# A modulation section summed on TensorE in four column groups instead of on VectorE

## The chip, the core and the metric

The kernel runs on one core of one Trainium2 chip. A core has five engines that run their own instruction streams in order: TensorE (PE in the profile; PEld is its loading of weights), VectorE (DVE), ScalarE (ACT), GpSimd (POOL) and SyncE (SP), which issues most DMAs. The metric is the device time of one execution, in microseconds.

## The reference

One decoder layer for 256 tokens of width 2048, batch 1, all in float32. Six vectors of 2048 numbers, shift, scale and gate for each of two halves, are made from a conditioning vector c ("the modulation"); this product with the 2048 x 12288 matrix `w_ada` is what the change touches.

```python
mod = einsum("bd,de->be", silu(c), w_ada) + b_ada
shift1, scale1, gate1, shift2, scale2, gate2 = split(mod, 6)
h = rms_norm(x, norm1_g) * (1 + scale1) + shift1
proj = einsum("bsd,de->bse", h, w_in)              # 73 column tiles of 128
lru_out = gelu(proj_gate) * rg_lru(conv(proj_x), ...)        # 32 of the tiles
ssd_out = mamba2_heads(proj_z, proj_xBC, proj_dt, ...)       # 41 of the tiles
mix = einsum("bse,ed->bsd", concat(lru_out, ssd_out), w_out)
x = x + gate1 * mix
h2 = rms_norm(x, norm2_g) * (1 + scale2) + shift2
x = x + gate2 * peer(h2, ...)                      # product keys, 16384 experts, top 16
out = rms_norm(x, final_norm_g)
```

`rg_lru` is a depthwise convolution, two small gate products per head and a scan along the tokens. `mamba2_heads` is a convolution, a chunked state-space scan in four groups of heads, and a gated norm.

## The kernel before, in words

Activations lie with features on the 128 partitions and tokens along the free axis. Every weight matrix comes from HBM as 512 KB blocks of 128 x 1024 numbers (`raw`, four buffers). ScalarE makes the rounded high part of a block (line 144), VectorE the low part, the block less its high part (line 153), both into `hl` (four buffers), and TensorE multiplies high and low parts. `issue_split` (line 139) queues ScalarE's part of one block and, one block behind, VectorE's, and after that the DMA of a further block on SP. It is called once after each half tile of products, so a block's split starts when TensorE has freed the buffer four blocks back.

The kernel runs in stages, on TensorE in this order:

1. Shift and scale of the first half of the layer (`ada_group`, line 250): 512 KB pieces of `w_ada` are the moving operand, `silu(c)` the stationary one. `cz` holds each column of `silu(c)` widened with zeros to 32 columns, and four products with four different 128-row pieces go to the four 32-row groups of one PSUM bank (line 257). ScalarE then copies the bank (line 266), and four products with a column of ones add up its rows and bring the result into column form (line 271). The first 12 tiles of the input projection run in between (`w_pass`).
2. The loop over the other 61 tiles of the input projection (line 795): 32 tiles of the SSD part first (slots 0 to 31), then 29 of the LRU part (slots 32 to 60). Each tile has two halves of 8 row blocks; tiles in which the high part of the weights meets both parts of `h` in one 512-column product use `wide` (lines 444 and 446), the others three products of 256 columns (lines 809 to 811).
3. The output projection: its first half by `w_out` rows (lines 869 to 871), its second half by column tiles (lines 915 and 916), with the first gate applied in `x2_evac` (line 838). Then the second norm, the query product, product keys and top 16, and the experts (a dense part by TensorE, the rest gathered by GpSimd).

The order of the side work is written by hand. `mid()` (line 170) runs once after each half tile and queues what was deferred for it; `bg_pop()` runs once after a tile and queues one step of the SSD or LRU work (its TensorE part at once, its elementwise part at the next `mid`). In the SSD part these steps are transposes, state and output products (lines 523 to 650), and in the first and middle tiles a softplus of many small VectorE instructions (lines 202 to 215); in the LRU part the gate products (line 663), the convolution (lines 417 and 421), scans (line 697) and gated outputs.

The other sections of the modulation are summed on VectorE while the projections run. `adq` (line 354) lists 96 steps: three sections (index 2, the first gate; 3 and 4, scale and shift of the second half), two halves of 1024 columns, 16 row blocks each. `ada_step` (line 373) multiplies one 128 x 1024 block of `w_ada` by a column of `silu(c)` and adds it to the running sum `adacc` (line 384; the first of a sum on line 381), then queues on SP the DMA of a further block (line 364; two buffers). After 16 steps, eight products with ones (line 393) bring the sum into column form two slots later. `ada_tick(rate, slot)` adds the rate to a counter and does one step for each whole number in it. It is called once for each tile of the loop from slot 1 on, with 0.65 in the SSD part and 1.1 in the LRU part, and 60 times in the output projection with 0.74. The last section, the second gate, is made later and is not touched.

Of the kernel before, what the change touches and what calls it, by code (L numbers as in the profile page):

```python
# [8 lines left out]
FT = mybir.dt.float32  # L9
# [5 lines left out]
AF = mybir.ActivationFunctionType  # L15
# [4 lines left out]
D = 2048  # L20
# [7 lines left out]
NRAW = 4  # L28
NHL = 4
GD = 3  # L30
ADA_SSD, ADA_LRU, ADA_OUT = 0.65, 1.1, 0.74

N0 = 12
NQ = 4
# [24 lines left out]
def hybrid_kernel(ctx, tc, xT, cols, w_ada, w_in, lru_w, w_o1, w_o2, w_q, keys, u_t, v_t, fng, out):  # L59
    nc = tc.nc  # L60
    pe, act, dve, pool, sp = nc.tensor, nc.scalar, nc.vector, nc.gpsimd, nc.sync
# [7 lines left out]
    mix = mixs.enter_context(tc.tile_pool(name="mix", bufs=1))  # L69

    def bank(n):
        return psum.tile([128, 512], FT, name=f"b{n}")
# [13 lines left out]
    def col(name, i=0, n=1):  # L86
        o, w = COLS[name]
        return cc[:, o + i:o + i + n]
# [3 lines left out]
    ones = const.tile([128, 128], FT, name="ones")  # L92
# [46 lines left out]
    def issue_split():  # L139
        n = st["split"]  # L140
        if n < len(items):
            r = raws.pop(n)
            t = wp.tile([128, 2, 1024], FR, name="hl", bufs=NHL)
            act.activation(t[:, 0], r, AF.Copy)  # L144
            hls[n] = t
            st["split"] += 1
            los.append((t, r))
        issue_lo(st["lag"] if n < len(items) else 0)
# [7 lines left out]
    def take():  # L156
        n = st["use"]
        st["use"] += 1
        return hls.pop(n)
# [7 lines left out]
    def defer(f, d=0):  # L167
        stages[d].append(f)

    def mid():  # L170
        fs = stages.pop(0)
        stages.append([])
        for f in fs:
            f()

    def bg_pop():
        for q in (bg, bg2):
            if q:
                pf, ef = q.pop(0)[:2]
                if pf:  # L180
                    pf()
                if ef:
                    defer(ef)
# [34 lines left out]
    cact = const.tile([128, 16], FT, name="cact")  # L218
# [9 lines left out]
    mod = const.tile([128, 6, 16], FT, name="mod")  # L228
# [122 lines left out]
            mid()  # L351


    adq = [(s, h, k) for s in (2, 3, 4) for h in range(2) for k in range(16)]
    ada = {"dma": 0, "use": 0, "acc": None, "bank": 6}
    adr = {}

    def ada_dma():
        n = ada["dma"]
        if n < len(adq):  # L360
            s, h, k = adq[n]
            adr[n] = mix.tile([128, 1024], FT, name="adr", bufs=2)
            o = {2: 2, 3: 4, 4: 3, 5: 5}[s] * D + h * 1024
            sp.dma_start(adr[n], w_ada[k * 128:(k + 1) * 128, o:o + 1024])
            ada["dma"] += 1
# [3 lines left out]
    def pe_due(slot):  # L369
        while pedue and pedue[0][0] <= slot:  # L370
            pedue.pop(0)[1]()

    def ada_step(slot):
        u = ada["use"]
        if u >= len(adq):
            return
        s, h, k = adq[u]
        w = adr.pop(u)
        if k == 0:
            ada["acc"] = mix.tile([128, 1024], FT, name="adacc", bufs=2)  # L380
            dve.tensor_scalar(ada["acc"], w, cact[:, 0:1], None, op0=OP.mult)
        else:
            a = ada["acc"]
            dve.scalar_tensor_tensor(a, w, cact[:, k:k + 1], a, op0=OP.mult, op1=OP.add)  # L384
        ada["use"] += 1
        ada_dma()
        if k == 15:
            a = ada["acc"]

            def fin():  # L390
                p = bank(ada["bank"])
                for i in range(8):
                    pe.matmul(p[:, i:i + 1], a[:, i * 128:(i + 1) * 128], ones[:, 0:1], start=True, stop=True)

                def add():
                    m = mod[:, s, 8 * h:8 * h + 8]
                    dve.tensor_add(m, p[:, :8], col("b_ada", 16 * s + 8 * h, 8))
                    if s == 3:
                        dve.scalar_tensor_tensor(m, m, 1.0, col("g2", 8 * h, 8), op0=OP.add, op1=OP.mult)
                defer(add)  # L400
            pedue.append((slot + 2, fin))
# [3 lines left out]
    def ada_tick(rate, slot):  # L405
        adt[0] += rate
        while adt[0] >= 1.0:
            adt[0] -= 1.0
            ada_step(slot)
# [32 lines left out]
    def wide(ps, w, kk, x, k):  # L442
        c = slice(kk * 128, (kk + 1) * 128)
        pe.matmul(ps, w[:, 0, c], x[:, k].rearrange("p a b -> p (a b)"), start=(k == 0), stop=False,  # L444
                  skip_group_check=True)
        pe.matmul(ps[:, :256], w[:, 1, c], x[:, k, 0], start=False, stop=(k == 15), skip_group_check=True)  # L446
# [276 lines left out]
    def lru_w_load():  # L723
        nonlocal nw
        if nw < 16:
            t = mix.tile([128, 2, 128], FT, name="wai", bufs=2)
            sp.dma_start(t, lru_w[nw])
            LR["w"][nw] = t
            nw += 1
# [57 lines left out]
    mid()  # L787
    mid()
    mid()
    for _ in range(2):  # L790
        ada_dma()
    for n in range(n2):
        w_pass(3, n, lambda e, ps: defer(lambda: evac(ETILES[e], ps)))
    slot = 0
    for e in ETILES[N0:]:
        ps = bank(slot % 3)
        two = e < 16 or 32 <= e < 48
        if not two:
            ps = ps[:, :256]
        for h in range(2):  # L800
            w = take()
            for kk in range(8):
                k = 8 * h + kk
                wh = w[:, 0, kk * 128:(kk + 1) * 128]
                wl = w[:, 1, kk * 128:(kk + 1) * 128]
                if two:
                    wide(ps, w, kk, hT, k)
                    continue
                pe.matmul(ps, wh, hT[:, k, 0, :], start=(k == 0), stop=False)  # L809
                pe.matmul(ps, wh, hT[:, k, 1, :], start=False, stop=False)  # L810
                pe.matmul(ps, wl, hT[:, k, 0, :], start=False, stop=(k == 15))  # L811
            issue_split()
            mid()
            if h == 0 and slot > 0:
                ada_tick(ADA_SSD if e >= 32 else ADA_LRU, slot)
        if e == 62:
            for _ in range(2):
                lru_w_load()
        bg_pop()
        ada["bank"] = 6 if slot >= 44 else (slot + 2) % 3  # L820
        pe_due(slot)
        defer(lambda e=e, ps=ps: evac(e, ps))
        slot += 1
# [38 lines left out]
    for n, k in enumerate(korder):  # L862
        w = take()
# [41 lines left out]
    for d in range(8, 16):  # L905
        ps = bank(3 + d % 2)
        for q in range(4):
            w = take()
            for kk in range(8):
                k = korder[8 * q + kk]  # L910
# [108 lines left out]
    for tb in range(2):  # L1019
        a = s1.tile([128, 1800], FT, name=f"ts{tb}")  # L1020
# [179 lines left out]
    for q in range(4):  # L1200
        w = [take() for _ in range(NQ // 2)]
        for kk in range(4):
            k = 4 * q + kk
# [11 lines left out]
    for e in range(NQ, 16):  # L1215
        p = bank(4 + e % 2)
# [381 lines left out]
```

## Time and profile before

| | |
|---|---|
| median of 3 runs | 2150.16 us (2148.74 to 2153.45) |
| the profiled execution | 2152.05 us, span 2150.3 us |
| input projection loop, SSD part | 147.2 to 366.0 us of the span |
| input projection loop, LRU part | 366.0 to 571.7 us |
| output projection and second norm | about 571.7 to 772 us |

The span runs from the first instruction of the program to the last; the execution's time has some 1.7 us around it. Three kinds of view are used below. In busy time by stretch, each engine has its busy microseconds and number of instructions in a stretch of the span; PEclk is TensorE's granted clock as a share of full speed, and the last two columns are the busy share of the DMA engines and the GB/s that they moved. In the timeline, a row is a start, a duration, an engine, the line in the kernel, the operation, and output and inputs by name; a number in square brackets is idle time of that engine just before, and what ended it. Rows of one line that follow each other are merged, with their count. Products overlap on TensorE, so a product's cost in a dense sequence is the distance between starts, not its duration. In the waits, a row names who waited for whom, with total, number and longest. A float32 product is two instructions in the profile.

### The profile page before, as it was taken

To read this page: it belongs to the slowest core of one execution; us is meant where nothing else is said; L and a number is where in the kernel's file an instruction comes from. 1 tells how busy PE (TensorE), PEld (TensorE's weight loads), DVE (VectorE), ACT (ScalarE), POOL (GpSimd) and SP (SyncE) were. 2 spreads that over 40 slices of the span, in tenths; PEclk is the share of its full clock that TensorE was granted. 3 is DMA by queue.
4 is the path that set the end of the run, shared out by engine and by line. 5 is a ranking of instruction groups with operands and counts; after the bars stand their busy time and mean duration, and the time that the engine had idled before them with its cause. 6 is when DMAs were issued, how large, how long until landed. Compare 5 with 4: busy or idle time off the path is not lost.

```text
span 2150.3 us, 34720 instructions
## 1 busy us (share of the span) xinstructions
PE 2074.9 (96%) x13028; PEld 1629.3 (76%) x13028; DVE 1396.2 (65%) x1995; ACT 965.7 (45%) x1468; POOL 886.2 (41%) x729
## 2 busy tenths in 40 slices
PE   7999999999999989999999999999999999999997
PEld 4789898988999888888788787766666656656663
DVE  2368887987878867879979996443343354344344
ACT  3346665666644454444345454333333333333332
POOL 0003243322212010000515661678777767767774
PEclk9999999999999999999999999999999999999998
DMA  9967666767789955568786778899999999999996
GB/s 371 387 235 251 214 213 229 255 222 257 260 289 322 344 175 174 190 222 268 241 264 225 243 252 280 279 368 351 340 364 352 359 353 342 374 368 359 355 355 241
DMA packets 250615, 620.54 MB, mean 289 GB/s; under 512 B 38024, under 2 KB 122168, under 8 KB 228152
## 3 DMA queue, kind: packets, MB, share of 16 engines
q1 hardware_dynamic: 188992, 387.76, 52.4%
q0 software_dynamic: 45056, 175.52, 22.0%
q10 hardware_dynamic: 16400, 55.06, 7.6%
q8 instruction: 102, 1.67, 0.3%
q14 instruction: 65, 0.53, 0.1%
HBM read 696.60 MB, written 14.72 MB: 331 GB/s over the span
## 4 chain that ended last, share of the span: by engine, by line
PE 62%; DVE 15%; DMA 13%; issue 5%; ACT 2%; POOL 1%; SPq 0%; POOLq 0%; DVEq 0%; ACTq 0%
PE b L444 11%; PE b L1436 10%; PE b L1350 9%; DVE hl L153 7%; PE b L446 5%; DMA raw<-in_w_in 4%; PE b L1276 3%; PE b L1278 3%; PE b L1277 3%; PE b L915 3%; DMA two<-in_w_ada 3%; DMA vq<-in_v_t,X 2%; DMA X<-ad,X 2%; PE b L809 2%; PE b L811 2%
## 5 line engine op out<-in xcount | busy, mean ns | idle before, releaser
L144 ACT ACTIVATE hl<-raw 128x1024 fp32r<-128x1024 f32 x594 | 628.4, 1059 | 1034.8 <-PE b L446 306.9
L153 DVE TENSOR_TENSOR hl<-raw,hl 128x1024 fp32r<-128x1024 f32 x594 | 765.1, 1298 | 110.5 <-ACT hl L144 109.7
L444 PE MATMUL b<-H,hl 128*128 128x512 f32 x1376 | 495.8, 403 | 3.1 <-DVE qT L450 2.7
L446 PE MATMUL b<-H,hl 128*128 128x256 f32 x1376 | 386.7, 281 | 3.7 <-DVE hl L153 3.6
L444 PEld LDWEIGHTS b<-H,hl 128*128 128x128 f32 x1376 | 259.2, 188 | 92.2 <-issue 26.3
L1329 POOL DMA_INDIRECT X<-ad,X x256 | 292.6, 1143 | 87.3 <-issue 74.0
L1436 PE MATMUL b<-hl,X 128*128 128x512 f32 x1152 | 273.8, 394 | 7.0 <-ACT X L437 5.2
L1436 PEld LDWEIGHTS b<-hl,X 128*128 128x128 f32 x1152 | 212.3, 188 | 81.7 <-issue 26.8
L446 PEld LDWEIGHTS b<-H,hl 128*128 128x128 f32 x1376 | 260.4, 189 | 6.0 <-DVE hl L153 5.3
L1276 PE MATMUL b<-hl,H 128*128 128x512 f32 x640 | 253.2, 396 | 0.0
L1278 PE MATMUL b<-hl,H 128*128 128x512 f32 x640 | 250.3, 391 | 3.0 <-DVE hl L153 3.0
L1277 PE MATMUL b<-hl,H 128*128 128x512 f32 x640 | 250.1, 391 | 0.0
L1320 POOL DMA_INDIRECT vq<-in_v_t,X x128 | 155.0, 1211 | 101.0 <-DVE vq L1490 43.4
L1320 POOL DMA_INDIRECT tk<-in_v_t,X x128 | 145.0, 1133 | 60.9 <-issue 21.1
L1340 DVE TENSOR_TENSOR Wz<-X 128x4 f32<-128x4 f32 x64 | 10.9, 171 | 241.8 <-ACT X L1336 187.7
L811 PE MATMUL b<-H,hl 128*128 128x256 f32 x560 | 160.8, 287 | 4.2 <-DVE hl L153 4.2
L809 PE MATMUL b<-H,hl 128*128 128x256 f32 x560 | 164.0, 293 | 0.0
L810 PE MATMUL b<-H,hl 128*128 128x256 f32 x560 | 160.5, 287 | 0.0
L1278 PEld LDWEIGHTS b<-hl,H 128*128 128x128 f32 x640 | 120.5, 188 | 29.8 <-DVE hl L153 4.5
L384 DVE SCALAR_TENSOR_TENSOR adacc<-adr,cact,adacc 128x1024 f32<-128x1024 f32 x90 | 128.1, 1424 | 20.6 <-DMA adr<-in_w_ada 20.5
L1276 PEld LDWEIGHTS b<-hl,H 128*128 128x128 f32 x640 | 120.4, 188 | 24.1
L1277 PEld LDWEIGHTS b<-hl,H 128*128 128x128 f32 x640 | 120.6, 188 | 23.7
(318 smaller groups left out, 3187.1 us busy)
## 6 DMA issues: line engine op xcount, KB each, us to landing
raw<-in_u_t SPq DMA_DIRECT2D x208, 512.0 KB, 4.7
raw<-in_w_in SPq DMA_DIRECT2D x146, 512.0 KB, 5.0
adr<-in_w_ada SPq DMA_DIRECT2D x96, 512.0 KB, 5.1
adw<-in_w_ada SPq DMA_DIRECT2D x64, 512.0 KB, 10.8
raw<-in_w_o SPq DMA_DIRECT2D x64, 512.0 KB, 5.6
raw<-in_u_t ACTq DMA_DIRECT2D x48, 512.0 KB, 7.2
raw<-in_v_t SPq DMA_DIRECT2D x48, 512.0 KB, 7.8
raw<-in_v_t ACTq DMA_DIRECT2D x48, 512.0 KB, 7.4
```

The source lines that it names most:

```text
L144: act.activation(t[:, 0], r, AF.Copy)
L153: dve.tensor_sub(t[:, 1], r, t[:, 0].bitcast(FT))
L444: pe.matmul(ps, w[:, 0, c], x[:, k].rearrange("p a b -> p (a b)"), start=(k == 0), stop=False, skip_group_check=True)
L446: pe.matmul(ps[:, :256], w[:, 1, c], x[:, k, 0], start=False, stop=(k == 15), skip_group_check=True)
L809: pe.matmul(ps, wh, hT[:, k, 0, :], start=(k == 0), stop=False)
L811: pe.matmul(ps, wl, hT[:, k, 0, :], start=False, stop=(k == 15))
L1276: pe.matmul(o, hh, w[:, 0, :, kk], start=(k == 0), stop=False)
L1277: pe.matmul(o, hl_, w[:, 0, :, kk], start=False, stop=False)
L1278: pe.matmul(o, hh, w[:, 1, :, kk], start=False, stop=(k == 15))
L1320: pool.indirect_dma_start(x, None, vf, bass.IndirectOffsetOnAxis(ap=eV[:, t:t + 1], axis=0), bounds_check=E1 - 1, oob_is_err=False)
L1329: pool.indirect_dma_start(wA[:, n:n + 1], None, adf, bass.IndirectOffsetOnAxis(ap=eW[:, t:t + 1], axis=0), bounds_check=T * E1 - 1, oob_is ...
L1436: pe.matmul(ob[tb * 2 + c], w[:, i, s], v[:, k, c * 512:(c + 1) * 512], start=(jj == 0 and (i, k) == (0, 0)), stop=(jj == JD - 1 and k == 1))
```

## The change

The first gate (index 2) leaves `adq`, which now has 64 steps for two sections, and is made by 16 steps on TensorE, one after the first half of each odd slot from 1 to 31. A step (`gate1_step`) does four products: a column of `silu(c)`, not widened, is the stationary operand, a 128 x 512 piece of `w_ada` the moving one, and each goes to one row of another 32-row group in bank 3, which VectorE clears once at the start. Four steps make 512 columns of the gate; then ScalarE copies the bank at the next half tile, four products with ones follow at the half tile after that in bank 4, and VectorE adds `b_ada`. The pieces are loaded two at a time by SP (512 KB each, 256 rows of 512 columns), two steps ahead, into the four buffers that `adr` and `adacc` have; the second load of the fourth step of each 512 columns waits for the products with ones. `ada_tick` is no longer called in the SSD part and has 0.7 instead of 1.1 in the LRU part; its first two loads go out at slot 31.

```diff
-ADA_SSD, ADA_LRU, ADA_OUT = 0.65, 1.1, 0.74
+ADA_LRU, ADA_OUT = 0.7, 0.74
...
-    adq = [(s, h, k) for s in (2, 3, 4) for h in range(2) for k in range(16)]
+    gp = {}
+
+    def gate1_load(n):
+        if n < 32:
+            q, r = divmod(n, 8)
+            gp[n] = mix.tile([128, 2, 512], FT, name="adp", tag=("adr", "adacc")[n // 2 % 2], bufs=2)
+            sp.dma_start(gp[n], w_ada[r * 256:(r + 1) * 256, 2 * D + q * 512:2 * D + (q + 1) * 512]
+                         .rearrange("(k p) d -> p k d", p=128))
+
+    def gate1_step(n):
+        q, c4 = divmod(n, 4)
+        if n == 0:
+            gp["b"] = bank(3)
+            dve.memset(gp["b"], 0.0)
+        w = [gp.pop(2 * n + i) for i in range(2)]
+        for g in range(4):
+            k = 4 * c4 + g
+            pe.matmul(gp["b"][32 * g:32 * g + 1, :], cact[:, k:k + 1], w[g // 2][:, g % 2],
+                      start=(c4 == 0), stop=(c4 == 3), skip_group_check=True)
+        if c4 < 3:
+            gate1_load(2 * n + 4)
+            gate1_load(2 * n + 5)
+            return
+        a = mix.tile([128, 512], FT, name="adrow", tag=("adr", "adacc")[n % 2], bufs=2)
+        gate1_load(2 * n + 4)
+
+        def cols_pe():
+            p = bank(4)
+            for i in range(4):
+                pe.matmul(p[:, i:i + 1], a[:, i * 128:(i + 1) * 128], ones[:, 0:1], start=True, stop=True)
+            gate1_load(2 * n + 5)
+            defer(lambda: dve.tensor_add(mod[:, 2, 4 * q:4 * q + 4], p[:, :4], col("b_ada", 32 + 4 * q, 4)))
+
+        def row():
+            act.activation(a, gp["b"], AF.Copy)
+            defer(cols_pe)
+        defer(row)
+
+    adq = [(s, h, k) for s in (3, 4) for h in range(2) for k in range(16)]
...
-    for _ in range(2):
-        ada_dma()
+    for n in range(4):
+        gate1_load(n)
...
             if h == 0 and slot > 0:
-                ada_tick(ADA_SSD if e >= 32 else ADA_LRU, slot)
+                if e < 32:
+                    ada_tick(ADA_LRU, slot)
+                elif slot % 2:
+                    gate1_step(slot // 2)
+                if slot == 31:
+                    for _ in range(2):
+                        ada_dma()
```

## The prediction

> **What bounds the kernel now.** I read the page first, for the span and the chain of work that ended last.
>
> ```profile
> span 2150.3 us, 34720 instructions
> ...
> PE 2074.9 (96%) x13028; PEld 1629.3 (76%) x13028; DVE 1396.2 (65%) x1995; ACT 965.7 (45%) x1468; POOL 886.2 (41%) x729
> ...
> PE 62%; DVE 15%; DMA 13%; issue 5%; ACT 2%; POOL 1%; SPq 0%; POOLq 0%; DVEq 0%; ACTq 0%
> ```
>
> TensorE (PE) is the bound: it is busy 96% of the span, and apart from its own weight loads (PEld) nothing passes 65%. So an edit that gives TensorE work costs its price at once, and one that takes work from VectorE (DVE) gains only where TensorE stands waiting for VectorE. How much that is must be read by stage. The next view is busy time by stretch: the SSD tiles of the projection loop before and after 181 us, the LRU tiles, and one stretch inside these.
>
> ```profile
> core 0: us, PE busy (x) PEld busy (x) DVE busy (x) ACT busy (x) POOL busy (x), PEclk, DMA share, GB/s
> 147.20:181.00 33.80, 30.09 (x217) 27.63 (x217) 31.05 (x50) 17.04 (x28) 8.98 (x10) 1.00 0.61 202
> 181.00:366.00 185.00, 180.85 (x1332) 166.71 (x1331) 155.18 (x221) 113.38 (x210) 61.38 (x55) 0.99 0.67 223
> 366.00:571.70 205.70, 196.25 (x1339) 181.05 (x1338) 173.74 (x201) 136.74 (x206) 49.49 (x32) 0.97 0.73 241
> 500.00:520.00 20.00, 16.65 (x105) 15.71 (x104) 19.82 (x22) 11.99 (x17) 8.90 (x3) 0.83 0.76 240
> ```
>
> TensorE's idle time is the first number less the PE number: 3.7 us, 4.2 us and 9.5 us in the three stages. The granted clock adds what TensorE loses while it counts as busy: 0.01 of 185 us is 1.9 us in the SSD part, 0.03 of 205.7 us is 6.2 us in the LRU. So the whole that a lighter VectorE could win is 6.1 us after 181 us in the SSD stage and 15.7 us in the LRU. The last row shows what the worst place looks like: VectorE busy 19.8 of 20 us, TensorE idle for 3.4 us of them and then at half clock for a while. The next rows show that place itself (VectorE's, then TensorE's timeline).
>
> ```profile
> 500.03 4.62 DVE L384 SCALAR_TENSOR_TENSOR adacc<-adr,cact,adacc 128x1024 f32<-128x1024 f32 x2
> ```
>
> ```profile
> 507.32 2.04 PE L663 MATMUL b<-xct,wai 128*128 128x256 f32 x4 [3.35 <-ACT xct L417]
> 508.81 0.78 PE L809 MATMUL b<-H,hl 128*128 128x256 f32 x1
> 509.38 0.41 PE L810 MATMUL b<-H,hl 128*128 128x256 f32 x1
> 509.59 0.41 PE L811 MATMUL b<-H,hl 128*128 128x256 f32 x1
> ```
>
> Two modulation steps stood back to back on VectorE, 4.6 us in all, with the weights' low parts and the convolution queued behind them; TensorE then waited 3.35 us, and its next products start 0.21 us apart where 0.12 us is usual (83.52 to 83.64 below). That is the loss the change could take away.
>
> **What is removed from VectorE.** Line 384's steps in the SSD stage and in the LRU, and all of them in the run (count: shortest/median/longest ns, first and last start):
>
> ```profile
> 147.20:366.00 218.80, 23.38 (x18) 0.99 0.66 219
> 366.00:571.70 205.70, 45.71 (x30) 0.97 0.73 241
> ```
>
> ```profile
> L384 DVE SCALAR_TENSOR_TENSOR adacc<-adr,cact,adacc x90: 1255/1278/3429, 181.1 to 755.6; 128x1024 f32<-128x1024 f32 x90
> ```
>
> By the code there are 31 x 0.65 = 20 steps in the SSD stage (18 here and two that open a sum, on line 381) and 29 x 1.1 = 32 in the LRU. After the change there are none and 29 x 0.7 = 20. So VectorE loses 23.4 us in the SSD stage and 12 x 45.71/30 = 18.3 us in the LRU. Both counts reach the output projection with 44 steps to go at the same 0.74, so I take that stage as unchanged. The first step of before starts at 181.1 us: the 3.7 us of idle time ahead of it are not the steps' doing and stay.
>
> What TensorE gets back of this: in the SSD stage at most 6.1 us. I take 4.5, since part of that idle time ends on ScalarE rather than on VectorE. In the LRU, the steps fall by 12 in 32, which of 15.7 us would be 5.9 if stalls went with their number; but a queue that overflows gives more than its share, and at 0.7 a tile no two steps come back to back (at 1.1 one tile in ten has two, as at 500 us). The upper end is all 15.7. I take 10, nearer the middle than the proportion because the largest stall is of the double kind.
>
> **What TensorE gets.** Sixteen steps of four products of a 128x512 block of weights, each to its own 32-row group of one PSUM bank. The kernel's start does the same with 32-column operands (line 257); TensorE's timeline shows two such steps in a row, and one alone among the projection's products:
>
> ```profile
> 77.39 1.92 PE L257 MATMUL b<-adw,cz 128*32 128x512 f32 x16
> 79.25 0.39 PE L319 MATMUL b<-H,hl 128*128 128x256 f32 x1
> ...
> 82.10 0.28 PE L322 MATMUL b<-H,hl 128*128 128x256 f32 x1
> 82.31 1.07 PE L257 MATMUL b<-adw,cz 128*32 128x512 f32 x8
> 83.30 0.38 PE L319 MATMUL b<-H,hl 128*128 128x256 f32 x1
> 83.52 0.28 PE L321 MATMUL b<-H,hl 128*128 128x256 f32 x1
> 83.64 0.28 PE L322 MATMUL b<-H,hl 128*128 128x256 f32 x1
> ```
>
> A lone step takes the start of the second product after it from 0.24 us (two spacings of 0.12) to 83.52 - 82.10 = 1.42 us behind the product before it: 1.18 us. Inside a run of steps the further one costs 79.25 - 77.39 less 83.30 - 82.31, 0.87 us. In the SSD stage each step stands alone, so 16 x 1.18 = 18.9 us (13.9 at the least price). The operand has one column instead of 32; nothing here shows a product with so narrow an operand, and I take the price of the 32-column one, the nearest row.
>
> The first two steps stand behind the loop's second and fourth tile, ahead of 181 us, where TensorE idles for 3.7 us anyway. I let one of them hide there: -1.2 (0 to -2.4). VectorE's memset of one bank falls in the same crowded stretch; it is in that range.
>
> Each quarter also needs a copy of a bank on ScalarE and four small sums on TensorE. The sums are 16 in all, as before, where two bursts of eight went:
>
> ```profile
> 562.16 1.68 PE b L393 x16
> ```
>
> ```profile
> L266 ACT ACTIVATE X<-b x8: 574/588/598, 21.3 to 126.8; 128x512 f32<-128x512 f32 x8
> ...
>   PE b L271: 3.5, 4
> ```
>
> Their number costs nothing new (two bursts of 1.68 us become four of half that). But they follow the copy by one tile half and wait for it if ScalarE is late. The start's eight copies (0.59 us each) made the sums wait in four cases, 3.5 us together. For four copies I bound it by 0 and 3.5 us and take 1.0, since ScalarE is 61% busy here (113.4 of 185) and half a tile lies between.
>
> **Loads.** SP's loads for the first gate now wait for TensorE to have read the buffer, instead of VectorE; behind them on SP stand the loads of projection weights. These have a later condition of their own:
>
> ```profile
> L144 ACT ACTIVATE hl<-raw 128x1024 fp32r<-128x1024 f32 x594 | 628.4, 1059 | 1034.8 <-PE b L446 306.9 <-PE b L1436 217.2 <-PE b L1278 147.0
> L153 DVE TENSOR_TENSOR hl<-raw,hl 128x1024 fp32r<-128x1024 f32 x594 | 765.1, 1298 | 110.5 <-ACT hl L144 109.7
> ```
>
> The next such load needs line 153 of a block whose line 144 itself waits for the end of the same tile half: 1.06 + 1.30 = 2.4 us after it, when the step of 1.18 us is done. So the wait costs nothing; without that cover, up to 1.2 us for each step. The SSD stage gets 32 loads of 512 KB where it had 20, two at a time and in shorter rows; its DMA share of 0.67 leaves room, and the LRU has 12 loads fewer.
>
> **The sum** against the profiled execution's own 2152.05 us (span 2150.3): 18.9 + 1.0 - 1.2 - 4.5 - 10 = +4.2, so 2156.2. That execution lies 1.9 us over the median of the runs, 2150.16; on the median it is 2154.4. Its own range is -1 to +10 around 2150.2. A measurement of this kernel can tell about 0.2%, 4.3 us, from no change, so the forecast stands on that line.
>
> **Rivals.** *VectorE's backlog vanishes (faster).* All that waits on VectorE after 181 us goes: 18.9 - 2.4 - 6.1 - 15.7 = -5.3, 2144.9; with steps at 0.87 us, -10.3, 2139.9. It decides if VectorE stays ahead through its long bursts in the LRU. For it: the 500 us row. Against: in the LRU VectorE stays at (173.7 - 18.3)/205.7, 76% busy. 22%.
>
> *The stalls move.* TensorE in the LRU waits for what stands behind gates and scans anyway: only 4 of 15.7 and 2 of 6.1 return and nothing hides: 18.9 + 1.0 - 6 = +13.9, 2164.1. For it: the wait at 507 us names ScalarE's convolution, not a modulation step. 13%.
>
> *The half-clock stretches stay.* They can come from TensorE's own bursts of tiny products, which remain:
>
> ```profile
> 337.02 1.92 PE L393 MATMUL b<-ones,adacc 128*128 128x1 f32 x16 [0.75 <-DVE zs L450]
> 339.13 0.42 PE L810 MATMUL b<-H,hl 128*128 128x256 f32 x1
> 339.34 0.42 PE L811 MATMUL b<-H,hl 128*128 128x256 f32 x1
> ```
>
> Here half-clock spacing (0.21) follows only 0.75 us of idle time and a burst of sums. If so, only the clock loss at 500 us, 0.17 of 20 us or 3.4 us, can go with the stalls: the pools shrink to 4.2 and 9.5 + 3.4 = 12.9 us, my shares of them to 3.1 and 8.2, and the sum is 18.9 + 1.0 - 1.2 - 3.1 - 8.2 = +7.4, 2157.6. 9%. The Trainium skill, "TensorE: Matmul & The Clock Gate" (HAM oscillation), says that TensorE falls to half clock after an idle gap of more than about 3.4 us. By that rule the dip after 507 us is explained and the one at 339 us, after 0.75 us, is not; the time by the rule is this rival's, and the trace agrees with it in one place and not in the other.
>
> *The four groups do not run side by side* with one-column operands: a step is 4 x 0.87 + 0.31 = 3.8 us, 16 of them 60.6, and the sum +45.9, 2196. 3%, since the 32-column form does run so. *Loads arrive late:* a pair, 1 MB at the LRU row's 241 GB/s, puts 4.4 us before a projection load; if each pair cost 0.5 us, +8 more, 2162.4. 3%.
>
> **Numbers.** Forecast 50%, rivals 22, 13, 9, 3 and 3. Of the forecast's half, 2 parts in 100 are faster by over 0.2%, 28 within, 20 slower. Faster: 22 + 2 = 24%. Within: 28%. Slower: 20 + 13 + 9 + 3 + 3 = 48%. The range runs from 2143, between the two ends of the first rival, to 2165, just over the second's 2164.1; outside lie about half of the first, a little of the second and the 2196.
>
> **What would show it.** In the new profile: sixteen groups on TensorE whose neighbours stand about 1.2 us further apart (wrong if near 3.8); no line-384 steps before the LRU and 20 in it; TensorE's idle time after the first tiles under 2 us in the SSD stage and near half of 9.5 us in the LRU, with a clock nearer 1.00; SSD tiles longer by about 14 us in all, LRU tiles shorter by about 10; the output projection unchanged. The forecast is wrong if the LRU gives back less than 6 or more than 14 us, or if SSD tiles wait for loads.

## The result and the profile after

The changed kernel takes 2167.43 us (median of 4 runs, 2165.92 to 2169.63) against 2151.05 us for the kernel before (4 runs beside it): a ratio of 1.006, with a 95% interval of 1.004 to 1.0079, so 9 to 17 us slower. The two medians lie 16.4 us apart (1.0076), at the upper end of that interval. Timed again later, the same pair gave 1.0075 (1.0056 to 1.0093). The profiled execution has a span of 2167.8 us where the kernel before had 2150.3.

The sign is the one forecast; the forecast of +4 us was too small. 2150.16 us times 1.006 is 2163, inside the range of 2143 to 2165 but near its upper end; the median itself lies above it. To see where the rest lies, I read the start of each tile's first product from TensorE's timeline, the same tile in both traces, and took the difference. A few of these starts, for every kernel of this study (us of the span; slot 2 is the loop's third tile, slot 32 the first LRU tile):

| kernel | slot 2 | slot 32 | output projection | first gathered product | end |
|---|---|---|---|---|---|
| before | 163.6 | 366.0 | 571.7 | 1366.0 | 2150.3 |
| changed | 171.9 | 385.9 | 583.6 | 1378.7 | 2167.8 |
| changed, again | 172.2 | 386.3 | 587.1 | 1383.2 | 2177.3 |
| clear_early | 165.2 | 379.6 | 579.9 | 1373.6 | 2167.2 |
| no_gate_sum | 163.6 | 357.9 | 555.7 | 1351.5 | 2147.1 |
| one_row | 166.3 | 420.1 | 620.0 | 1415.7 | 2213.7 |
| steps_in_pairs | 163.5 | 378.3 | 577.6 | 1370.9 | 2165.4 |
| rates_only | 165.5 | 376.3 | 583.0 | 1376.3 | 2169.1 |
| even_rates | 163.4 | 370.0 | 575.6 | 1371.7 | 2169.7 |
| push_out | 163.6 | 366.6 | 564.9 | 1375.9 | 2171.4 |
| sum_bank | 163.9 | 364.3 | 570.2 | 1364.1 | 2144.7 |
| sum_bank_even | 165.7 | 365.9 | 567.1 | 1362.2 | 2148.9 |
| sum_bank_85 | 163.7 | 367.5 | 568.3 | 1364.6 | 2151.1 |

The changed kernel loses 8.4 us in one tile, the second. From there to the first LRU tile it loses 11.7 more, in jumps of 1.1 or 1.2 us at the tiles that hold a step and of 0.9 at those with column sums, less some 8 us that come back at slots 16 to 18 and 26 to 28; in the LRU it wins another 8 back. At the start of the output projection it is 11.9 us behind, at the first gathered product 12.7, and at the end 17.5.

The tile with the 8.4 us first. TensorE's timeline of the changed kernel there (line 371 is the new step, lines 482 and 484 are the projection's products, 444 and 446 before; the x8 of a step are four products of two instructions each, while a product of the projection is one):

```profile
159.04 0.28 PE L484 MATMUL b<-H,hl 128*128 128x256 f32 x1
165.97 1.88 PE L371 MATMUL b<-adp,cact 128*1 128x512 f32 x8 [6.64 <-DVE b L367]
167.78 0.80 PE L482 MATMUL b<-H,hl 128*128 128x512 f32 x1
168.38 0.41 PE L484 MATMUL b<-H,hl 128*128 128x256 f32 x1
168.59 0.63 PE L482 MATMUL b<-H,hl 128*128 128x512 f32 x1
```

and VectorE's, in which nothing ahead of the clearing shows idle time:

```profile
160.21 1.51 DVE L459 SCALAR_TENSOR_TENSOR X<-b,hcw,X 128x255 f32<-128x255 f32 x3
161.64 1.22 DVE L153 TENSOR_TENSOR hl<-raw,hl 128x1024 fp32r<-128x1024 f32 x1
162.77 0.82 DVE L523 TENSOR_TENSOR dtt<-dtt 128x128 f32<-128x128 f32 x1
163.51 0.41 DVE L472 SCALAR_TENSOR_TENSOR X<-stmp,b 128x256 f32<-128x256 f32 x1
163.84 1.48 DVE L153 TENSOR_TENSOR hl<-raw,hl 128x1024 fp32r<-128x1024 f32 x1
165.43 0.48 DVE L367 MEMSET b<- 128x512 f32 x1
165.83 1.20 DVE L153 TENSOR_TENSOR hl<-raw,hl 128x1024 fp32r<-128x1024 f32 x1
```

The clearing takes 0.48 us. But it stands in VectorE's queue behind some six microseconds of convolutions, low parts and small products. TensorE reaches the first step after the product at 159.04 and stands still until the clearing is done. Then the step itself lasts 1.88 us, and products behind it start 0.21 us apart (168.38 to 168.59) where 0.12 is usual: half clock.

Now the stages, by busy time in the same stretches as before: the first two tiles, the rest of the SSD part, the LRU part, the output projection and norm.

```profile
core 0: us, PE busy (x) PEld busy (x) DVE busy (x) ACT busy (x) POOL busy (x), PEclk, DMA share, GB/s
147.10:171.90 24.80, 15.21 (x96) 11.69 (x94) 20.65 (x36) 8.88 (x16) 7.43 (x8) 0.86 0.53 178
171.90:385.90 214.00, 214.00 (x1588) 184.13 (x1587) 142.84 (x220) 122.79 (x225) 55.69 (x57) 1.00 0.69 232
385.90:583.60 197.70, 191.44 (x1330) 176.43 (x1329) 153.15 (x183) 137.67 (x208) 45.96 (x32) 0.99 0.65 216
583.60:783.70 200.10, 195.30 (x1374) 182.18 (x1372) 157.06 (x153) 92.51 (x113) 31.68 (x20) 0.99 0.86 306
```

From the third tile on the SSD part has no idle time on TensorE (214.00 of 214.00 us) and a clock of 1.00: all that VectorE had cost there is back, and still the part is longer, by the price of the steps and the wait of the second tile. In the LRU part 6.3 us of idle time and a clock of 0.99 (2.0 us) remain, 8.3 us where before had 15.7.

A lone step in a quiet place, the second one, on TensorE's timeline:

```profile
180.47 0.28 PE L484 MATMUL b<-H,hl 128*128 128x256 f32 x1
180.68 1.04 PE L371 MATMUL b<-adp,cact 128*1 128x512 f32 x8
181.65 0.50 PE L482 MATMUL b<-H,hl 128*128 128x512 f32 x1
181.98 0.28 PE L484 MATMUL b<-H,hl 128*128 128x256 f32 x1
```

It holds TensorE about as long as the step at the kernel's start did. The column sums never waited for ScalarE's copy; in the view of their line the changed kernel lists no wait:

```profile
L383 PE MATMUL b<-ones,adrow x32: 164/250/250, 217.3 to 389.7; 128*128 128x1 f32 x32
its engine sat idle before it (us, times) until:
who waited for it (us, times):
```

### The profile page after: what moved, and what is told of

Same layout as the page of the kernel before. It is cut to its first block, busy times and chain, and to the rows that moved or that the text cites. A ratio compares the mean times of both kernels' runs of the same rounds, so it can differ in the third digit from the quotient of the medians.

```text
span 2167.8 us, 34926 instructions
## 1 busy us (share of the span) xinstructions
PE 2091.2 (96%) x13156; PEld 1627.3 (75%) x13156; DVE 1350.8 (62%) x1966; ACT 966.2 (45%) x1472; POOL 871.6 (40%) x729
## 4 chain that ended last, share of the span: by engine, by line
PE 44%; DVE 11%; DMA 10%; issue 4%; POOL 1%; ACT 1%; SPq 0%; POOLq 0%; DVEq 0%; ACTq 0%
PE b L1480 9%; PE b L1394 8%; PE b L482 8%; DVE hl L153 5%; PE b L484 4%; PE b L1320 3%; PE b L1322 3%; PE b L1321 3%; DMA X<-ad,X 3%; DMA two<-in_w_ada 2%; PE b L959 2%; DMA tk<-in_v_t,X 2%; DMA adr<-in_w_ada 2%; DMA vq<-in_v_t,X 1%; PE b L960 1%
## 5 line engine op out<-in xcount | busy, mean ns | idle before, releaser
L153 DVE TENSOR_TENSOR hl<-raw,hl 128x1024 fp32r<-128x1024 f32 x594 | 756.4, 1284 | 126.9 <-ACT hl L144 126.4
L1364 POOL DMA_INDIRECT vq<-in_v_t,X x128 | 146.2, 1142 | 101.9 <-DVE vq L1534 39.1
L1394 PE MATMUL b<-tk,Wz 128*32 128x512 f32 x1024 | 117.9, 601 | 5.2 <-DVE Wz L1384 5.2
```

The costliest lines, as they stand in the source:

```text
L153: dve.tensor_sub(t[:, 1], r, t[:, 0].bitcast(FT))
L1364: pool.indirect_dma_start(x, None, vf, bass.IndirectOffsetOnAxis(ap=eV[:, t:t + 1], axis=0), bounds_check=E1 - 1, oob_is_err=False)
L1394: pe.matmul(sb[c][32 * g:32 * g + 32, :], Wz[:, x:x + 32], vs[4 * (q % 2) + g][:, c * 512:(c + 1) * 512], start=(m == 0), stop=(m == 31), ...
```

## The experiments

The experiments ran in three sets, each on one chip, three chips in all: first clear_early, no_gate_sum, one_row and rates_only, then steps_in_pairs, changed_again, even_rates and push_out, last the three sum_bank kernels. The kernel before, run in each set, had medians of 2166.66, 2164.25 and 2152.53 us, so each kernel is given as a ratio to it in the same set, and the place of a gain or loss is taken from the trace, against the one trace of the kernel before. In the loop that holds well: push_out, which starts like the kernel before, repeats its tile starts within 0.1 us up to slot 26.

**clear_early**: the clearing stays at the second tile, the sixteen steps come one tile later (and VectorE's first two loads, at slot 32).

```diff
-        if n == 0:
-            gp["b"] = bank(3)
-            dve.memset(gp["b"], 0.0)
...
+                if slot == 1:
+                    gp["b"] = bank(3)
+                    dve.memset(gp["b"], 0.0)
...
-                elif slot % 2:
-                    gate1_step(slot // 2)
+                if slot <= 32 and slot % 2 == 0:
+                    gate1_step(slot // 2 - 1)
...
```

Expected: 

> Bank 3 is cleared where the changed kernel clears it (second tile), but the sixteen TensorE steps begin one tile later, at even slots 2 to 32. Theory (TensorE stands 6.6 us behind the clearing, which is queued behind VectorE's backlog): the loss of 8.4 us at the second tile shrinks to about the 1.1 us of any other step, so 2167.4 - 7.2 = 2160, between 2158 and 2162. Rival (VectorE is late there anyway and TensorE would wait for weights instead): 2165 to 2168.

Measured: 1.0025 (1.0008 to 1.0043). The second tile loses nothing against the kernel before, and the third, which now holds the first step, 1.2 us:

```profile
168.00 0.28 PE L846 MATMUL b<-H,hl 128*128 128x256 f32 x1
168.21 1.04 PE L368 MATMUL b<-adp,cact 128*1 128x512 f32 x8
169.18 0.38 PE L844 MATMUL b<-H,hl 128*128 128x256 f32 x1
169.41 0.28 PE L845 MATMUL b<-H,hl 128*128 128x256 f32 x1
```

The second product after the step starts 1.41 us behind the product before it, 1.17 us more than two spacings. The clearing itself still stands in VectorE's queue at its place (from 167.47 us in this trace, whose loop began 1.5 us later); only TensorE no longer meets it, by 0.3 us: the clearing ends at 167.95, the step starts at 168.21. So the theory holds: the wait, not VectorE's work, was the loss, and TensorE would not have waited there for weights. The expected 2160 is a ratio of 1.0042 to 2151, which the interval just holds. Counted from the loop's start, the trace is 5.3 us ahead of the changed kernel's at the output projection where 7.2 were expected; 0.5 us of the rest is a wait for ScalarE's copy at slot 33. The kernel is still slower than before.

**no_gate_sum**: the first gate's sums are left out; the gate is its bias alone.

```diff
-    for n in range(4):
-        gate1_load(n)
+    dve.tensor_copy(mod[:, 2, :], col("b_ada", 32, 16))
...
-                elif slot % 2:
-                    gate1_step(slot // 2)
```

Expected: 

> The changed kernel without the first gate's sums: no loads, no TensorE steps, no column sums; the gate is its bias alone. Leaves out that part of the computation. Theory (VectorE's relief is worth what the traces of before and after show behind the steps: 4.8 us in the SSD stage and 8.5 us in the LRU, and 3.4 us of column sums go): 2151 - 16.7 = 2134, between 2130 and 2139. Rival (the relief alone is worth the whole pools of 6.1 and 15.7 us, and TensorE's steps ate part of it): 2126 or less. Rival (stalls only move): 2143 or more.

Measured: 0.9897 (0.9873 to 0.9921). In the trace it is 8.1 us ahead of the kernel before at the first LRU tile and 16.0 at the output projection, against 16.7 expected; the ratio says 17 to 27 us. So the relief of VectorE is worth 8 us in each part, a burst of column sums (1.7 us) in each included, and no more: the first rival falls by the trace, the second by both. Its LRU part moves tile by tile as the changed kernel's does: from slot 35 to slot 60 both win 7 to 8 us, with the same single jumps of 4.1 us at slot 51, 1.6 at slot 52 and 3.9 at slot 59. TensorE's steps thus do not touch the LRU's gain.

**one_row**: all products of a quarter go to one row, so no two can run side by side. Nothing is cleared, and the column sums read one row.

```diff
-            dve.memset(gp["b"], 0.0)
...
-            pe.matmul(gp["b"][32 * g:32 * g + 1, :], cact[:, k:k + 1], w[g // 2][:, g % 2],
-                      start=(c4 == 0), stop=(c4 == 3), skip_group_check=True)
+            pe.matmul(gp["b"][:1, :], cact[:, k:k + 1], w[g // 2][:, g % 2],
+                      start=(k == 0), stop=(k == 15), skip_group_check=True)
...
```

Expected: 

> The changed kernel with all sixteen products of a quarter added into one row of the bank, one after the other, instead of into four row groups; nothing to clear, and the column sums read one row. Theory (the four groups run side by side, a product alone costs 0.86 us): a step costs 4 x 0.86 + 0.3 = 3.7 us instead of 1.1, +42 us for sixteen, less 7.2 us for the clearing: 2202, between 2195 and 2210. Rival (one-column products to different groups do not overlap): 2160.

Measured: one run, 2215.42 us beside a median of 2166.66 for the kernel before, +49 (the expectation, 2202 against 2151, was +51); in the trace it is 48.3 us behind at the output projection. A step:

```profile
191.50 0.28 PE L848 MATMUL b<-H,hl 128*128 128x256 f32 x1
191.71 3.59 PE L370 MATMUL b<-adp,cact 128*1 128x512 f32 x8
195.23 0.39 PE L846 MATMUL b<-H,hl 128*128 128x256 f32 x1
195.45 0.28 PE L847 MATMUL b<-H,hl 128*128 128x256 f32 x1
```

195.45 - 191.50 less 0.24 is 3.7 us, as expected. So the four groups of the changed kernel do run side by side with one-column operands. This run shows one thing more: its first step stands where the changed kernel's does, with nothing to wait for, and the third tile starts only 2.7 us later than before (166.3 for 163.6). So 1.0 us of that step hides in idle time.

**steps_in_pairs**: clear_early with two steps together at every fourth slot.

```diff
-                if slot <= 32 and slot % 2 == 0:
-                    gate1_step(slot // 2 - 1)
+                if slot <= 30 and slot % 4 == 2:
+                    gate1_step(slot // 2 - 1)
+                    gate1_step(slot // 2)
```

Expected: 

> The early-cleared kernel with its sixteen TensorE steps two at a time, eight pairs at every fourth slot. Theory (a lone step pays about 0.31 us for going into the narrow-column products and back, the second of a pair only 0.87 us): a pair costs 2.0 to 2.1 us instead of 2.3, so 2 us less in all than the early-cleared kernel, ratio near 1.002. Rival (the loads, four at a time, come too late, or delay the projection's): one or more pairs or the halves after them wait, ratio over 1.004.

Measured: 1.0033 (1.0017 to 1.005), not told apart from clear_early by time. In the trace a pair costs 2.0 us (slots 2, 6, 10, 14: +2.0, +2.1, +2.0, +2.0) where two lone steps cost 2.3, and no pair waited for a load. The price of going in and out is as read: at slot 34, counted from the loop's start, the trace is 2.0 us ahead of clear_early's. At the output projection only 0.4 of that is left, after a loss of 2.4 us at slot 46 that clear_early does not have; 2 us are too little for the time to show.

**changed_again**. Expected: 

> The changed kernel, unaltered, timed again beside the others. Its trace stood 12.5 us behind that of before at the start of the gathers and 17.4 us at the end, with no instruction changed in between. Theory (the last 4.9 us are the gathers' own spread, not the change's): ratio 1.0058, between 1.0045 and 1.007, and between 1350 us and the end no constant difference to the kernels beside it. Rival (the late part is the change's too): 1.008.

Measured: 1.0075 (1.0056 to 1.0093). This does not settle it by time, since the interval holds both figures. The traces help: in these two sets every kernel loses between the first gathered product and the end, where all have the same instructions, against the trace of before (clear_early 9.3 us, rates_only 8.5, push_out 11.2, no_gate_sum 11.3), even the one that is ahead. That part varies by itself, by more than the 4.8 us in question. In its own set the changed kernel's, 794.1 us, is the shortest of four (794.5, 795.5 and 798.0), which speaks against the rival; but the kernel before was not traced there. This trace also stands 3.5 us further behind at the output projection than the first one of the same kernel, most of it 1.6 us at slot 39, 0.7 at slot 46 and 0.8 less gain at slot 51; so a trace of the same program can differ by that much there. The 12 to 15 us up to the output projection are the change's; whether any of the last 5 is stays open.

**rates_only** and **push_out** ask whether the LRU's gain can be had without TensorE.

```diff
-ADA_SSD, ADA_LRU, ADA_OUT = 0.65, 1.1, 0.74
+ADA_SSD, ADA_LRU, ADA_OUT = 1.02, 0.7, 0.74     # rates_only
+ADA_SSD, ADA_LRU, ADA_OUT = 0.65, 0.7, 0.94     # push_out
```

Expected (rates_only): 

> The kernel before with all three sections on VectorE, but 1.02 steps a tile in the SSD part and 0.7 in the LRU part (31.6 + 20.3 steps there, as many as before in all; the output projection unchanged). Theory (the LRU's gain comes from its rate alone): the LRU part gets 8 us shorter as in the changed kernel; the SSD part carries 12 more steps of 1.28 us, VectorE busy some 202 of 219 us, and gets 3 to 8 us longer: 2146 to 2152. Rival (SSD part overloaded): more than 2155. Rival (the LRU's gain needs the loads or the phase of the change): LRU part not shorter, 2155 or more.

Expected (push_out): 

> The kernel before with 0.65, 0.7 and 0.94: the LRU part as light as in the changed kernel, and the twelve steps it loses go into the output projection instead of onto TensorE. Theory (the LRU's 8 us depend on VectorE's rate there and on nothing that TensorE does): LRU part 7 to 9 us shorter; the output projection, where DMA engines are busy 0.87 of the time, takes twelve more loads of 512 KB and gets 6 to 14 us longer; ratio 0.999 to 1.003. Rival (there is room in the output projection): it gets less than 4 us longer, ratio 0.996 to 0.998.

Measured: rates_only 1.0022 (1.0005 to 1.0038), push_out 1.0023 (1.001 to 1.0037). In push_out the LRU part is 7.4 us shorter (198.3 for 205.7), with VectorE alone: the theory on the LRU holds, though 1.7 us of it is a burst of column sums that this rate moves out of the part. The output projection gives it back and more. The stretch from there to the end of the norm, push_out:

```profile
564.90:779.00 214.10, 201.36 (x1390) 185.87 (x1388) 173.28 (x166) 92.33 (x113) 29.18 (x20) 0.98 0.90 313
```

It is 14.8 us longer at the norm, with waits for loads: ScalarE stood 41.3 us for `w_out` blocks (18.9 in the trace of before). So there is no room, and the upper bound of the expectation was just passed. rates_only comes out on the side of its rivals (1.0022 times 2151 is 2155.7). Its SSD part loses 8.3 us from slot 16 to slot 32, but the LRU part is not shorter (206.7 us): it has the gain from slot 51 on, and a loss of 9.2 us at slots 34 and 35 that no theory had. The waits of rates_only by TensorE in the LRU part name it:

```profile
PE b L393 <- DVE xct L421: 4.2, 1, 4.2
PE b L811 <- DVE hl L153: 2.1, 2, 1.4
```

Line 393 are the column sums of a finished half section. They go to the bank of the tile two slots on (line 820), and if VectorE has not emptied it (line 421 is a convolution), TensorE waits for VectorE's queue, as at the clearing.

**even_rates**: 0.75 and 1.0, so that no tile has two steps.

Expected: 

> The kernel before with 0.75 and 1.0 steps a tile instead of 0.65 and 1.1: three steps move from the LRU part into the SSD part, and no LRU tile has two. Theory (what the changed kernel won in the LRU was mostly the pair of steps behind which the gate product at 507 us waited 3.35 us, and the half clock after it): LRU part 4 to 8 us shorter, SSD part 0 to 4 longer, ratio 0.997 to 1.000. Rival (the gain needs the lower rate): LRU part shorter by 2 us or less, ratio 1.000 to 1.003.

Measured: 1.0017 (1.0003 to 1.003), the rival's side. The trace shows the LRU gain of 4.1 us at slot 51, and against it +8.2 us at slots 24 and 25 and +10.4 at slots 42 and 43, of which 6.3 come back at the next two. TensorE's waits again name the sums:

```profile
PE b L393 <- DVE ggt L450: 5.0, 1, 5.0
PE b L393 <- DVE zs L450: 3.1, 1, 3.1
```

Three kernels test that: the sums go to banks that nobody has to empty.

```diff
-        ada["bank"] = 6 if slot >= 44 else (slot + 2) % 3
-        pe_due(slot)
+        ada["bank"] = 6 if slot >= 44 else 4
+        if slot < 34 or slot >= 44:
+            pe_due(slot)
```

**sum_bank** (rates as before). Expected: 

> The kernel before with its rates, but the column sums of VectorE's sections go to bank 4 in the SSD part, and those due in slots 34 to 43 wait until slot 44, for bank 6; before, they went to the bank of the tile two slots on, which VectorE may still have to empty. Theory (a column sum is dear only where TensorE meets a bank not yet emptied, as for 0.75 us at 337 us in the trace of before): 1 to 3 us less around slot 27, nothing else, ratio 0.9985 to 1.000. Rival (the bank is no matter): 1.000 and no change around slot 27.

Measured: 1.0005 (0.9992 to 1.0018); 2.3 us less at slots 27 and 28 in the trace, 1.6 at the output projection; the sums no longer wait, and no half clock follows them. As expected, and too little for the time to show.

**sum_bank_even** (0.75 and 1.0). Expected: 

> The same banks with 0.75 and 1.0 steps a tile. Theory (of the run with these rates alone, 8.2 us at slots 24 and 25 and 10.4 us at slots 42 to 44, of which 6.3 came back, were TensorE waiting for a bank, and the rates themselves win in the LRU): no jump at these slots, start of the output projection 5 to 9 us ahead of the kernel before, ratio 0.996 to 0.998. Rival (the rates win nothing, the waits were VectorE's backlog): 1.000 or more.

Measured: 0.9973 (0.996 to 0.9985), the fastest complete kernel here, 4.6 us ahead at the output projection, just short of the 5 expected (6.4 from slot 0 on, as its loop began 1.8 us late). Slots 24 and 25 lose 1.8 instead of 8.2 us, slots 42 and 43 nothing instead of 10.4. In the view of its line, the waits for other tiles' banks are gone; what is left is the end of the section's own sum:

```profile
its engine sat idle before it (us, times) until:
  DVE adacc L384: 2.7, 2
```

**sum_bank_85** (0.85 and 0.9). Expected: 

> The same banks with 0.85 and 0.9 steps a tile, six steps moved from the LRU part to the SSD part. Theory (the LRU wins with each step less, the SSD part loses only in its softplus and first LRU tiles): start of the output projection 4 to 10 us ahead of the kernel before, ratio 0.9955 to 0.998. Rival (the SSD part has no room): slots 16 to 20 lose 5 us or more, as with 1.02, ratio 1.000.

Measured: 0.9983 (0.997 to 0.9996), 3.4 us ahead at the output projection, just under what was expected. Six moved steps win hardly more in the LRU than three (4.9 us and 4.5), and the SSD part loses 1.4.

## Why the prediction was right and wrong

- **The step that failed** is the clearing, which was priced at nothing of its own: "VectorE's memset of one bank falls in the same crowded stretch; it is in that range" (0 to -2.4). With it the first TensorE step was to cost 0 net (1.18 less 1.2 of hiding) and cost 8.4 us. The hiding itself was nearly right: one_row, which clears nothing, hides 1.0 us. The stretch was read rightly as crowded, and that was taken as cover; but all 3.7 us of TensorE's idle time there were waits for VectorE's low parts (line 153). The change put a new instruction at the end of just that late queue and made TensorE wait for it, 6.64 us, with a stretch of half clock behind. The bound had to be the delay of VectorE's queue in that place, which the trace of before shows (VectorE's timeline, then the one wait of TensorE there):

```profile
160.32 1.51 DVE L421 SCALAR_TENSOR_TENSOR X<-b,hcw,X 128x255 f32<-128x255 f32 x3
161.75 1.21 DVE L153 TENSOR_TENSOR hl<-raw,hl 128x1024 fp32r<-128x1024 f32 x1
162.88 0.28 DVE L485 TENSOR_TENSOR dtt<-dtt 128x128 f32<-128x128 f32 x1
163.45 0.42 DVE L434 SCALAR_TENSOR_TENSOR X<-stmp,b 128x256 f32<-128x256 f32 x1 [0.28 <-ACT stmp L429]
164.40 1.46 DVE L153 TENSOR_TENSOR hl<-raw,hl 128x1024 fp32r<-128x1024 f32 x1 [0.53 <-ACT hl L144]
```

```profile
160.46 0.39 PE L446 MATMUL b<-H,hl 128*128 128x256 f32 x1 [0.77 <-DVE hl L153]
```

TensorE ends the first half of the tile at 159.3 us, and the queue reaches the place of the clearing, behind the last row, at 165.9: 6.6 us could have been read before. Most of what VectorE does there TensorE needs only later, so before it waited 0.77 us. clear_early takes the wait of 6.64 us away, and the second tile loses nothing.
- **TensorE's price** was right: 1.18 us for a lone step was read, 1.1 to 1.2 are in the trace, and 2.0 for a pair. The one-column operand costs what the 32-column one did. one_row shows that side by side was needed: 3.7 us without.
- **The wait for ScalarE's copy** was put at 1.0 us and was none (0.5 us, once, in clear_early and in steps_in_pairs).
- **What VectorE gives back in the SSD part**: 4.5 of 6.1 us were taken; all came back (TensorE without idle time, clock 1.00). no_gate_sum shows the same 8 us, of which 1.7 are a burst of column sums that went.
- **In the LRU part** 10 of 15.7 us were taken; 7.4 came back (15.7 to 8.3). By tiles, 5.7 us come at slots 51 and 52, behind the double step, as reasoned; even_rates has the same 4.1 us at slot 51 with three steps moved. Another 5.0 us come at slots 59 and 60, a place that the prediction does not name. There the trace of before has a wait of 1.0 us for ScalarE, a burst of column sums (562 us) and half clock behind it; in the changed kernel that burst stands at slot 56, costs 1.6 us and has no half clock behind it. That it needs none of TensorE's steps is shown by push_out and no_gate_sum. That it is the rate alone is not: the rate also sets where the bursts fall. The half-clock stretches of the loop, four in the trace of before and, last, the one of the changed kernel's LRU part (the clock is the third figure from the end):

```profile
338.80:342.20 3.40, 3.40 (x18) 3.40 (x18) 3.40 (x7) 0.00 (x0) 0.54 (x1) 0.51 0.79 236
458.30:461.70 3.40, 3.40 (x12) 2.92 (x13) 3.40 (x6) 2.86 (x4) 0.00 (x0) 0.50 0.87 270
506.10:512.90 6.80, 5.58 (x22) 5.25 (x23) 6.73 (x10) 1.38 (x2) 2.03 (x1) 0.50 0.66 231
564.10:567.50 3.40, 3.40 (x18) 3.40 (x18) 3.33 (x6) 0.25 (x1) 0.00 (x0) 0.50 0.81 246
479.90:483.30 3.40, 3.40 (x13) 2.92 (x12) 3.40 (x7) 1.31 (x3) 0.00 (x0) 0.51 0.84 276
```

- **The sum**: 8.4 for the first step and its wait, 15 x 1.13 = 17.0 for the others, 0.2 for four short bursts of sums (0.9 each) in place of two of 1.7, less the 6.1 and 7.4 that came back, is 12.1; the trace has 11.9. Against the forecast's 4.2, the first step alone is +8.4; the rest cancel within 1 us. That the range still holds the ratio is luck: its upper end was set by the second rival, whose mechanism did not come.
- **Rivals.** That VectorE's backlog vanishes held in the SSD part and for half of the LRU. What came back, 13 to 14 us, is less than the 18 us of TensorE's steps, so the kernel would not have been faster even without the wait. That the stalls move was near in size (+13.9) and not in kind: it had 2 and 4 us coming back where 6 and 7 did, and the new wait is another. The half-clock rival was right on the cause in part: three of the four stretches of before (338.8, 458.3 and 564.1 us) begin at a burst of column sums or within 1 us behind it. The fourth begins at 506.1 us, when TensorE had stood for 2.1 of its 3.35 us. It was wrong that they stay: no burst of the changed kernel's loop has one. Groups ran side by side, and loads did not come late.
- **The late 5 us** behind the first gathered product were not in the forecast, which held everything there unchanged. Whether they are the change's is open.

## What to carry to other kernels

An engine that looks merely busy can be several microseconds behind without harm, as long as what it makes is buffered; the first instruction of which another engine needs the result at once then costs that whole lag, however short it is (6.64 us here for 0.48 us of work). So for each new wait look up how late the waited-for queue is at that place, put a clearing or a bank's emptying well ahead, and give short sums a bank that no one must empty. Work moved to the engine that bounds the kernel is paid in full (18 us here); spreading the same work more evenly on the engine it was on, once its short waits were gone, won 0.27% (0.15 to 0.4).

## What the runs showed of the hardware

Three things I had not expected. A product whose stationary operand has a single column, sent to its own 32-row group, is as cheap as with 32 columns: the four products of a step overlap, and a step holds TensorE 1.1 to 1.2 us, against 3.7 us when all write one row. TensorE's granted clock falls to half without a long idle time: at 458.3 us in the trace of before after 0.08 us of it in the 3.4 us ahead, with 1.84 us of column sums (sixteen instructions, 128x1), and at 479.9 us in the changed kernel after a wait of 1.76 us. Other such bursts have no half clock behind them (557 us in the changed kernel); what decides is not shown here. And the part that gathers rows by indirect DMA has its own spread: the same instructions, from the first gathered product to the end, took 784 us in the trace of before and 789 in the first of the changed kernel, 793 to 798 us in the eight traces of the first two sets of experiments, and 781 to 787 us in the three of the last set. Whether that goes with the chip or with the time is not shown. It hides differences of a few microseconds elsewhere.
